# A two-layer trunk on one core: the down projections of the FFNs as products on the upper and the lower 64 rows of the array, each half with a PSUM bank of its own

## The chip, the cores and the metric

The kernel runs on one core of one Trainium2 chip. The metric is the time of one execution on the device in microseconds (us); of several runs the median is given. The core has four engines that matter here: TensorE (PE in the profile, its weight loads PEld) multiplies, VectorE (DVE) and ScalarE (ACT) work on tiles, and the DMA queue of SyncE (SP) brings weights from DRAM. TensorE writes only to PSUM, which has eight banks of 128 partitions x 512 float32 values.

## What is computed

A decoder trunk of two layers on 256 tokens of width 2048. Layer 0 mixes tokens by window means, layer 1 by latent attention; each layer ends with a SwiGLU FFN with a hidden width of 5632. All is float32. Cut to the part that the change touches:

```python
D_MODEL, SEQ, DEPTH = 2048, 256, 2
FFN_DIM = ((8 * D_MODEL // 3 + 255) // 256) * 256        # 5632

def swiglu(h, w_gate, w_up, w_down):
    return (jax.nn.silu(h @ w_gate) * (h @ w_up)) @ w_down

def reference(x, c, ...):
    for i in range(DEPTH):
        ...
        h = modulate(rmsnorm(x, norm_ffn[i]), shift_f, scale_f)
        x = x + gate_f[:, None, :] * swiglu(h, ffn_gate[i], ffn_up[i], ffn_down[i])
    return rmsnorm(x, final_norm)
```

## The kernel before

**Products.** Every matrix of weights is cut into units of 512 rows x 512 columns (1 MB). A unit is loaded into a buffer `raw`, split by ScalarE into a rounded upper part `hi` (line 368, type float32r) and by VectorE into the rest, `lo` (line 370). Activations are held as an upper and a lower part too. `proj_unit` (lines 387 to 393) then forms upper times upper, lower times upper and upper times lower: 3 parts x 4 row tiles of 128 x 2 tiles of 128 tokens = 24 products, each with a weight load of 128 x 128 (the activations) and 512 streamed columns (the weights of the network). The two token tiles have one bank each. In the last unit of a sum, the products of the first token tile go before those of the second; in all others they alternate.

**Banks.** All banks come from one pool of eight buffers, `ps`, and are given out as they come free.

**The FFN.** The hidden width is 11 chunks of 512. `FFN_STEPS` (line 52) is the order: `p` projects a chunk through gate and up, `t` transposes it (line 587) and splits it (lines 590 and 591), `d` sends a group of chunks through the down projection. The groups are [0, 1, 2], [3, 4, 5], [6, 7, 8] and [9, 10]; step d0 is followed at once by two transposing steps, d1 and d2 by the projection of a chunk, and d3 ends the FFN. Step `d` is `down(i)` (lines 594 to 625): for each of four blocks of 512 columns it takes two banks, adds the units of the group's chunks to them and evacuates them: in d0 ScalarE copies a bank to `x` (line 623), in d1 and d2 VectorE adds it to `x` (line 625), and in d3 it goes through `StreamEnd` to the gate and the residual sum.

**What runs beside.** Each split calls `tick`, which now and then emits a unit of "background": rows of the adaLN matrices, loaded into a `raw` buffer and summed by VectorE (lines 183 and 233). In the first FFN that is about three background units for four units of weights, in the second fewer. At times a finished background sum is folded (line 261) or spread as a gate over four banks (lines 299 and 300) by TensorE, in between the units. Splits have a raised priority in the scheduler that orders each engine's queue; each queue runs strictly in order. There are six `raw` buffers and six for `hi` and `lo` together, so three units of split weights.

Of the kernel before, what the change touches and what calls it, by code (L numbers as in the profile page):

```python
# [17 lines left out]
P = 128  # L18
# [31 lines left out]

# an FFN's order: chunk projected (p), turned (t), group of chunks through the down projection (d)
FFN_STEPS = "p0 p1 t0 p2 t1 p3 t2 p4 p5 d0 t3 t4 p6 t5 d1 p7 t6 p8 t7 p9 t8 d2 p10 t9 t10 d3".split()
GROUPS = ([0, 1, 2], [3, 4, 5], [6, 7, 8], [9, 10])
# chunks begun block by block, and the chunk before which the residual stream leaves for DRAM
BEGUN = 6
ASIDE = 5
# row tiles of the first gate that the tensor engine sums
GM_PE = (8, 10, 12, KD - 2, KD - 1)
# units of weights over which the background of a stage is spread
FFN0_UNITS, MLA_UNITS, HEAD_UNITS, WO_UNITS, FFN1_UNITS = 95, 6, 16, 8, 60  # L60
# of the background: blocks left to the last FFN, units left to attention, units of the last FFN's first block
# that go ahead of the output projection
LATE, MLA_LATE, WO_LATE = 3, 9, 3
# splits of weights that go before the end of a fold, or of a gate
FOLD_WAIT, GATE_WAIT = 2, 1
# [27 lines left out]
def tile_trunk(ctx: ExitStack, tc: tile.TileContext, a: dict, out: bass.AP):  # L93
# [33 lines left out]

    # constants and small vectors
    x = const.tile([P, NT, D], F32, name="x")
# [32 lines left out]

    # adaLN rows: acc[p, n] = sum over row tiles of w[kt*128+p, n] * silu(c); partition 0 starts at the bias
    cols = const.tile([P, 10, KD], F32, name="cols")
# [20 lines left out]

    # a gate on all partitions, with some of its row tiles summed on the idle tensor engine
    class SharedPart(Part):
# [13 lines left out]

    # the same for CH columns of shift and scale at once, two row tiles in a unit
    class BlockPart:
# [39 lines left out]
        def add_sums(self, i, rows, ones_, first, last):  # L243
            """Adds the sums over partitions of rows [..., CH] to KL columns of a bank, which only its first product clears."""
            for k in range(KL):
                n = i * KL + k
                pe.matmul(self.sums[:, n:n + 1], lhsT=rows[:, k * P:(k + 1) * P], rhs=ones_, start=first and k == 0,
                          stop=last and k == KL - 1)
# [3 lines left out]
    def folded(acc, n, fin):  # L252
        """Sums over partitions of acc [P, n]: column 32 * b + i is in row 32 * r + i of column b, for any r."""
        tr = raw_t([P, n])
        dve.transpose(tr, acc)
        part = acc[:, :n // 32]
        dve.tensor_reduce(out=part, in_=tr.rearrange("p (b j) -> p b j", j=32), axis=AX.X, op=ALU.add)

        def finish():
            pt = ps_t()  # L260
            pe.matmul(pt[:, :n // 32], lhsT=fold, rhs=part, start=True, stop=True)  # L261
            v = pt[:, :n // 32].rearrange("p (k r) -> p k r", r=4)
            for r in range(4):
                rows = slice(32 * r, 32 * r + 32)
                fin(v[rows, :, r], rows)
        pending.append((FOLD_WAIT, finish))
# [21 lines left out]
    def gate_to(name):  # L288
        def done(acc):
            # both parts of the sums, split exactly like the weights  # L290
            hi, lo = gate_t([P, D], F32R), work.tile([P, D], F32R, tag="acc", bufs=2, name=nm("acc"))
            act.activation(hi, acc, AF.Copy)
            dve.tensor_tensor(out=lo, in0=acc, in1=hi.bitcast(F32), op=ALU.subtract)

            def finish():
                banks = [ps_t() for _ in range(ND)]
                for j in range(ND):
                    js = slice(j * CH, (j + 1) * CH)
                    pe.matmul(banks[j], lhsT=ones_r, rhs=hi[:, js], start=True, stop=False)  # L299
                    pe.matmul(banks[j], lhsT=ones_r, rhs=lo[:, js], start=False, stop=True)  # L300
                gates[name] = gate_t([P, D])
                for j in range(ND):
                    act.activation(gates[name][:, j * CH:(j + 1) * CH], banks[j], AF.Copy)
            pending.append((GATE_WAIT, finish))
        return done
# [19 lines left out]

    # units of the background for a unit of weights
    rate, credit, goal = [0.0], [0.0], [10 ** 6]
# [3 lines left out]
    def hold():  # L331
        """Emit no more of the background until release()."""
        held[0] = True
# [13 lines left out]
    def plan(left, units):  # L347
        """Spread the background down to what is left over the next units of weights."""
        pump(len(background) - goal[0])
        goal[0], credit[0] = left, 0.0  # L350
        rate[0] = (len(background) - left) / units if units else 0.0

    # what follows a unit of weights, queued behind the split of the next unit, which is more pressing
    def flush(*ins):
# [7 lines left out]

    # weights: a unit of 512 rows and 512 columns, split exactly into two parts of 12 bits
    def split(r, shape):
# [22 lines left out]
    def proj_unit(banks, t_, hi, lo, first, last, toks=range(NT)):  # L387
        """Adds a unit to the banks; the products with the lower part of the weights, which is split last, come last."""
        for part in [[tok] for tok in toks] if last else [toks]:
            order = [(w, i, k, tok) for w, i in ((hi, 0), (hi, 1), (lo, 0)) for k in range(KL) for tok in part]  # L390
            for n, (w, i, k, tok) in enumerate(order):
                pe.matmul(banks[tok], lhsT=t_[:, i, k, tok * P:(tok + 1) * P], rhs=w[:, k, :],  # L392
                          start=first and n < len(part), stop=last and n >= len(order) - len(part))

    def proj(src, tiles):
# [5 lines left out]

    # statistics of the residual stream
    ssq = [None]
# [71 lines left out]

    # while an FFN runs, the residual stream waits in DRAM and x gathers the FFN's sum before the gate
    aside = {}
# [55 lines left out]

    # a projection of the hidden state, begun before all of the hidden state is known
    class Begun:
# [36 lines left out]
    def ffn(l, hT, gate_name, begun, then):  # L572
# [21 lines left out]
        def down(i):  # L594
# [6 lines left out]
            for j in range(ND):  # L601
                js = slice(j * CH, (j + 1) * CH)
                banks = [ps_t() for _ in range(NT)]
                if last and j == ND - 1:
# [9 lines left out]
                for c in g:  # L614
                    hi, lo = w_unit(wd[c * CH:(c + 1) * CH, js])
                    proj_unit(banks, mids[c], hi, lo, c == g[0], c == g[-1])
                    if last and j == ND - 1 and c == g[0]:
                        then()
                for tok in range(NT):
                    if last:  # L620
                        end.piece(banks[tok], tok, j)
                    elif i == 0:
                        act.activation(x[:, tok, js], banks[tok], AF.Copy)
                    else:
                        dve.tensor_tensor(out=x[:, tok, js], in0=banks[tok], in1=x[:, tok, js], op=ALU.add)  # L625

# [16 lines left out]

    # rope tables with the rows of two heads on partitions; the sine has the sign of its half
    cos_t = const.tile([P, T], F32, name="cos_t")
# [31 lines left out]
    def rope_start(bank):  # L677
        """bank [128, T] holds the rows of two heads; returns what rope_end needs."""
        t_ = t2k([P, 2, T])
# [10 lines left out]

# [1 line left out]
    rope_tables()  # L692
# [19 lines left out]
    pump(KD)  # L712
    # window means less the values, of the normed stream and of a constant one
    flat = hl_t([P, len(WINDOWS), T], F32)
# [15 lines left out]

# [1 line left out]
    def sf_block(l, j, cshift, cscale, shared=False):  # L732
# [17 lines left out]
    def start_ffn(l, rstd, first, cshift, cscale, late):  # L750
        """The first chunks, block by block of the hidden state, as its shift and scale become known."""
        begun = begin(l, range(BEGUN), (0,))
# [88 lines left out]

# [1 line left out]
    pts = turned_pieces(scaled(rstd, 0, True))  # L843
# [56 lines left out]
    def keys_values(g):  # L900
        """Keys and values of four heads."""
        mem = act_t([P, 2 * KG * T], F32)
# [30 lines left out]

    # rope key, once with zeros below and once with zeros above, for both heads of a pair
    krT = const.tile([P, 2, T], F32, name="krT")
# [112 lines left out]
    for o in heads:  # L1048
        o.finish()
    # the first columns of the output projection fill the waits of the last pairs of heads  # L1050
    w_o, ob = a["w_o"][0], []
# [39 lines left out]

# [1 line left out]
    hT, begun = start_ffn(1, rstd, None, C_SF1, C_AF1, LATE)  # L1093
# [25 lines left out]
```

## Time and profile before

| | |
|---|---|
| median of 3 runs | 1966.45 us (1965.64 to 1966.51) |
| span of the profiled execution, first to last instruction | 1962.3 us |
| mean granted clock of TensorE | 0.983 |
| bytes moved by DMA | 572.66 MB, 292 GB/s on average |
| products of line 392 | 7008, in both FFNs, the attention and its projections |
| evacuations in d0 (line 623) | 16, of 0.60 us |
| evacuations in d1 and d2 (line 625) | 32, of 0.69 us |

The runs give the time of a whole execution; of the profiled one only the span between its first and last instruction is known. In the trace a product of TensorE lasts longer than the distance to the next one, since products are pipelined: what counts is the distance between starts. A merged row of the timeline gives the start of the first instruction of a run of like ones, the time from there to the end of the last, and their count. A row of a group gives busy time and mean duration, and behind the second bar the time for which the engine stood idle just before such instructions, with what ended most of it.

The down steps d0, d1 and d2 of the first FFN end near 520, 633 and 832 us of the span, those of the second near 1554, 1664 and 1864 us.

### The profile page before, as it was taken

The page shows a single profiled execution, that of the slowest core. Times are in us where ns is not written, and L with a number is a line of the kernel's source. Part 1 is how long each engine was busy: PE and PEld are TensorE (multiplying, and loading weights), DVE is VectorE, ACT ScalarE, POOL GpSimd, SP SyncE. Part 2 cuts the span into 40 slices and gives each one's busy share as a digit, 9 for nine tenths or more (in the row PEclk, how much of TensorE's full clock was granted, in tenths as well). Part 3 has the DMA queues.
Part 4 walks back from the last instruction along what each step waited for, and adds up shares of the span by engine and source line. Part 5 has one row for each costly group of instructions (what it writes and reads, how often), then busy time and mean ns, then how long its engine had stood idle before and what let it go on. Part 6 is the DMA issues. An engine that isn't in the chain of part 4 may idle for free. (4 is left out here: it accounts for less than half of the span.)

```text
span 1962.3 us, 21516 instructions
## 1 busy us (share of the span) xinstructions
PE 1853.0 (94%) x8485; PEld 1520.7 (77%) x8485; DVE 1546.4 (79%) x1312; ACT 850.0 (43%) x939; POOL 35.9 (2%) x33
## 2 busy tenths in 40 slices
PE   0489999999999999998999999999999999999998
PEld 0444888888888888886789987888888888888886
DVE  7887899998778778888989975889986566554556
ACT  3123544444443333334676744544444433343333
POOL 1000000000000000000000000000000000000000
PEclk9889999999999999999899999999999999999999
DMA  9999998898898989987888684989887667665561
GB/s 377 408 378 365 379 321 305 310 350 327 313 329 302 332 325 345 338 333 284 307 311 304 228 295 142 360 303 325 297 293 260 225 229 257 235 209 186 195 219 70
DMA packets 225184, 572.66 MB, mean 292 GB/s; under 512 B 11958, under 2 KB 16286, under 8 KB 203442
## 3 DMA queue, kind: packets, MB, share of 16 engines
q1 hardware_dynamic: 225084, 571.30, 80.9%
q8 instruction: 66, 1.08, 0.2%
q14 instruction: 34, 0.28, 0.0%
HBM read 564.97 MB, written 6.29 MB: 291 GB/s over the span
## 5 line engine op out<-in xcount | busy, mean ns | idle before, releaser
L392 PE MATMUL ps<-hl,act 128*128 128x512 f32 x7008 | 1609.5, 391 | 4.7 <-ACT act L459 2.2
L392 PEld LDWEIGHTS ps<-hl,act 128*128 128x128 f32 x7008 | 1315.1, 188 | 279.3 <-ACT act L459 4.4
L370 DVE TENSOR_TENSOR hl<-raw,hl 128x2048 fp32r<-128x2048 f32 x296 | 676.2, 2289 | 239.9 <-ACT hl L368 236.1
L368 ACT ACTIVATE hl<-raw 128x2048 fp32r<-128x2048 f32 x296 | 566.4, 1919 | 608.7 <-PE ps L392 542.1
L183 DVE SCALAR_TENSOR_TENSOR acc<-raw,s_col,acc 128x2048 f32<-128x2048 f32 x155 | 364.0, 2348 | 4.2 <-DMA raw<-in_mod_w_dram 1.6
L233 DVE SCALAR_TENSOR_TENSOR acc<-raw,s_col,acc 128x1024 f32<-128x1024 f32 x121 | 155.0, 1281 | 8.7 <-DMA raw<-in_mod_w_dram 7.2
L556 DVE TENSOR_TENSOR act<-ps,act 128x512 f32<-128x512 f32 x96 | 64.6, 687 | 14.1 <-PE ps L392 13.7
L275 PE MATMUL ps<-ones,acc 128*128 128x1 f32 x64 | 13.9, 352 | 62.8 <-DVE acc L183 39.9
L410 ACT ACTIVATE junk<-x 128x512 bf16<-128x512 f32 x40 | 25.2, 630 | 89.6 <-DVE x L526 44.1
L275 PEld LDWEIGHTS ps<-ones,acc 128*128 128x128 f32 x64 | 13.8, 332 | 64.5 <-DVE acc L183 41.4
L590 ACT ACTIVATE act<-ps 128x512 fp32r<-128x512 f32 x44 | 23.8, 596 | 61.5 <-PE ps L587 53.4
L625 DVE TENSOR_TENSOR x<-ps,x 128x512 f32<-128x512 f32 x32 | 22.1, 691 | 35.4 <-PE ps L392 35.4
L458 ACT ACTIVATE t2k<-ps,cols 128x256 f32<-128x256 f32 x64 | 33.2, 567 | 21.6 <-PE ps L444 17.0
L634 ACT ACTIVATE t2k<-ps 128x512 f32<-128x512 f32 x24 | 14.2, 593 | 64.2 <-PE ps L392 64.2
L918 PE MATMUL ps<-act,hl 128*128 128x256 f32 x128 | 37.2, 291 | 0.6 <-DVE hl L370 0.6
L919 PE MATMUL ps<-act,hl 128*128 128x256 f32 x128 | 36.7, 287 | 0.0
L920 PE MATMUL ps<-act,hl 128*128 128x256 f32 x128 | 36.1, 286 | 0.0
L591 DVE TENSOR_TENSOR act<-ps,act 128x512 fp32r<-128x512 f32 x44 | 28.2, 685 | 8.1 <-ACT act L590 8.0
L638 DVE TENSOR_TENSOR t2k<-ps,t2k 128x512 f32<-128x512 f32 x24 | 16.6, 690 | 21.3 <-PE ps L392 21.3
L444 PE MATMUL ps<-con,t2k 128*128 128x128 f32 x144 | 22.5, 306 | 11.2 <-DVE t2k L432 8.1
L784 PE MATMUL ps<-act,act 128*128 128x512 f32 x64 | 30.7, 644 | 0.9 <-issue 0.9
L554 ACT ACTIVATE act<-ps 128x512 f32<-128x512 f32 x32 | 19.1, 598 | 28.3 <-PE ps L392 28.1
(168 smaller groups left out, 955.0 us busy)
## 6 DMA issues: line engine op xcount, KB each, us to landing
raw<-in_mod_w_dram SPq DMA_DIRECT2D x128, 1024.0 KB
raw<-in_ffn_gate_dram SPq DMA_DIRECT2D x88, 1024.0 KB
raw<-in_ffn_up_dram SPq DMA_DIRECT2D x88, 1024.0 KB
raw<-in_ffn_down_dram SPq DMA_DIRECT2D x88, 1024.0 KB
raw<-in_mod_w_dram SPq DMA_DIRECT2D x128, 512.0 KB
raw<-in_kv_mod_w_dram SPq DMA_DIRECT2D x32, 1024.0 KB
raw<-in_w_o_dram SPq DMA_DIRECT2D x16, 1024.0 KB
raw<-in_w_uq_dram SPq DMA_DIRECT2D x8, 768.0 KB
```

The lines of the kernel that those rows point to most:

```text
L183: dve.scalar_tensor_tensor(out=self.acc, in0=r, scalar=s_col[:, self.kt:self.kt + 1], in1=self.acc, op0=ALU.mult, op1=ALU.add)
L233: dve.scalar_tensor_tensor(out=self.acc, in0=r[:, k], scalar=s_, in1=self.acc, op0=ALU.mult, op1=ALU.add)
L368: hi_ins = act.activation(hi, r, AF.Copy)
L370: lo_ins = dve.tensor_tensor(out=lo, in0=r, in1=hi.bitcast(F32), op=ALU.subtract)
L392: pe.matmul(banks[tok], lhsT=t_[:, i, k, tok * P:(tok + 1) * P], rhs=w[:, k, :], start=first and n < len(part), stop=last and n >= len(ord ...
L458: act.activation(full, pts[k // 2][:, k % 2, :], AF.Identity, scale=scale, bias=bias)
L556: dve.tensor_tensor(out=part, in0=banks[tok], in1=part, op=ALU.add)
L591: dve.tensor_tensor(out=m[:, 1, :, ts_], in0=v, in1=m[:, 0, :, ts_].bitcast(F32), op=ALU.subtract)
L784: pe.matmul(pt, lhsT=pooled[g // 2][:, g % 2, k, tok * P:(tok + 1) * P], rhs=wp[g][:, k, :], start=k == 0, stop=k == KL - 1)
L918: pe.matmul(pt[:, h, :], lhsT=wl(h0 + h, k), rhs=t_[:, 0, k, :], start=k == 0, stop=False)
L919: pe.matmul(pt[:, h, :], lhsT=wh(h0 + h, k), rhs=t_[:, 0, k, :], start=False, stop=False)
L920: pe.matmul(pt[:, h, :], lhsT=wh(h0 + h, k), rhs=t_[:, 1, k, :], start=False, stop=k == KL - 1)
```

## The change

A new helper, `half_rows_unit`, forms the same 24 products of a unit as 48: each is cut into the upper and the lower 64 of its 128 rows, and each half is summed in a bank of its own. `down` uses it for all groups but the last (d0, d1 and d2 of both FFNs); its blocks then hold four banks instead of two. The sum of the two halves is formed at the evacuation: in d0 ScalarE copies the bank of the upper half and VectorE adds that of the lower, in d1 and d2 VectorE adds both. The order by token tiles in the last unit of a sum is not kept there. The step d3, the projections and the attention keep `proj_unit`. Some comments are dropped as well, which shifts no instruction; later line numbers move by up to 14 lines.

```diff
+    def half_rows_unit(banks, t_, hi, lo, first, last):
+
+        order = [(w, i, k) for w, i in ((hi, 0), (hi, 1), (lo, 0)) for k in range(KL)]
+        for n, (w, i, k) in enumerate(order):
+            for tok in range(NT):
+                for half in range(2):
+                    rows = slice(half * P // 2, (half + 1) * P // 2)
+                    pe.matmul(banks[tok][half], lhsT=t_[rows, i, k, tok * P:(tok + 1) * P], rhs=w[rows, k, :],
+                              start=first and n == 0, stop=last and n == len(order) - 1)
...
             for j in range(ND):
                 js = slice(j * CH, (j + 1) * CH)
-                banks = [ps_t() for _ in range(NT)]
+                halves = not last
+                banks = [[ps_t() for _ in range(2)] if halves else ps_t() for _ in range(NT)]
...
                 for c in g:
                     hi, lo = w_unit(wd[c * CH:(c + 1) * CH, js])
-                    proj_unit(banks, mids[c], hi, lo, c == g[0], c == g[-1])
+                    unit = half_rows_unit if halves else proj_unit
+                    unit(banks, mids[c], hi, lo, c == g[0], c == g[-1])
                     if last and j == ND - 1 and c == g[0]:
                         then()
                 for tok in range(NT):
                     if last:
                         end.piece(banks[tok], tok, j)
-                    elif i == 0:
-                        act.activation(x[:, tok, js], banks[tok], AF.Copy)
-                    else:
-                        dve.tensor_tensor(out=x[:, tok, js], in0=banks[tok], in1=x[:, tok, js], op=ALU.add)
+                        continue
+                    for half, bank in enumerate(banks[tok]):
+                        if i == 0 and half == 0:
+                            act.activation(x[:, tok, js], bank, AF.Copy)
+                        else:
+                            dve.tensor_tensor(out=x[:, tok, js], in0=bank, in1=x[:, tok, js], op=ALU.add)
```

TensorE's queue where the first down step of the first FFN begins, before (`ps` are banks, `hl` the split weights, `act` the activations, which are loaded as the array's weights):

```order
L392 MATMUL ps_2683<-hl_2687,act_2157 128x512 x4
L392 MATMUL ps_2718<-hl_2725,act_2357 128x512 [waits Activation_49]
L392 MATMUL ps_2719<-hl_2725,act_2357 128x512 [waits DVE_49]
L392 MATMUL ps_2718<-hl_2725,act_2357 128x512
L392 MATMUL ps_2719<-hl_2725,act_2357 128x512
```

and now:

```order
L392 MATMUL ps_2683<-hl_2687,act_2157 128x512 x4
L402 MATMUL ps_2718<-hl_2727,act_2357 128x512 [waits Activation_49]
L402 MATMUL ps_2719<-hl_2727,act_2357 128x512 [waits DVE_49]
L402 MATMUL ps_2720<-hl_2727,act_2357 128x512 [waits DVE_49]
L402 MATMUL ps_2721<-hl_2727,act_2357 128x512 [waits DVE_49]
L402 MATMUL ps_2718<-hl_2727,act_2357 128x512
```

Two banks in turn have become four: upper and lower half of the first token tile, then of the second. The kind of product changes from whole to half rows at the first of these and stays until something else is queued between. The program order has 8 such switches in the first FFN (into and out of d0, d1 and d2, and twice more around the gate's products, which stand inside the last block of d0) and 6 in the second.

TensorE's queue at the end of d0 in the first FFN now; `t2k` are the chunks to be transposed:

```order
L402 MATMUL ps_3251<-hl_3394,act_2544 128x512
L402 MATMUL ps_3252<-hl_3394,act_2544 128x512
L597 MATMUL ps_3450<-con,t2k_2504 128x128 [waits Activation_49]
L597 MATMUL ps_3450<-con,t2k_2504 128x128 x3
L597 MATMUL ps_3457<-con,t2k_2506 128x128 [waits Activation_49]
L597 MATMUL ps_3457<-con,t2k_2506 128x128 x3
L597 MATMUL ps_3465<-con,t2k_2596 128x128 [waits Activation_49]
```

The transposes follow the last half product directly, and their banks wait for ScalarE.

VectorE's queue at the end of the first block of d2 in the first FFN, before (line 370 is a split, 183 a background sum, 498 the gate on a part of `x`):

```order
L183 SCALAR_TENSOR_TENSOR acc_4614<-raw_4804,s_col,acc_4614 128x2048 [waits DMAHW6_49,DVE_49]
L625 TENSOR_TENSOR x<-ps_4734,x 128x512 [waits PE_49]
L498 TENSOR_TENSOR x<-x,gate_3084 128x512 [waits DVE_49]
L625 TENSOR_TENSOR x<-ps_4735,x 128x512 [waits PE_49]
L370 TENSOR_TENSOR hl_4842<-raw_4839,hl_4841 128x2048 [waits DMAHW7_49,Activation_49]
```

and now (line 639 is the addition):

```order
L183 SCALAR_TENSOR_TENSOR acc_5222<-raw_5814,s_col,acc_5222 128x2048 [waits DMAHW0_49,DVE_49]
L639 TENSOR_TENSOR x<-ps_5342,x 128x512 [waits PE_49]
L639 TENSOR_TENSOR x<-ps_5344,x 128x512 [waits PE_49]
L639 TENSOR_TENSOR x<-ps_5343,x 128x512 [waits DVE_49]
L639 TENSOR_TENSOR x<-ps_5345,x 128x512 [waits DVE_49,PE_49]
L370 TENSOR_TENSOR hl_5642<-raw_5636,hl_5641 128x2048 [waits DMAHW2_49,Activation_49]
```

Four additions stand where two stood, the upper halves of both token tiles ahead of the lower ones, and the next split is queued behind them.

## The prediction

> **What bounds the kernel now.** First the page's busy times, then the six stretches of the trace in which the changed products run.
>
> ```profile
> PE 1853.0 (94%) x8485; PEld 1520.7 (77%) x8485; DVE 1546.4 (79%) x1312; ACT 850.0 (43%) x939; POOL 35.9 (2%) x33
> L392 PE MATMUL ps<-hl,act 128*128 128x512 f32 x7008 | 1609.5, 391 | 4.7 <-ACT act L459 2.2
> L392 PEld LDWEIGHTS ps<-hl,act 128*128 128x128 f32 x7008 | 1315.1, 188 | 279.3 <-ACT act L459 4.4
> ```
>
> TensorE carries the time: products of line 392 alone are 1609.5 us of the 1962.3 us span, and they waited 4.7 us in all. VectorE is second with 79%. An average says nothing of a stage, so here are the down steps whose groups are not the last, three per FFN (columns: stretch, its length, busy time and count of PE, PEld, DVE, ACT, POOL, then granted clock, DMA share, GB/s).
>
> ```profile
> 455.00:520.00 65.00, 65.00 (x288) 53.81 (x287) 50.47 (x24) 27.65 (x23) 3.63 (x2) 1.00 0.85 316
> 567.00:632.50 65.50, 65.50 (x292) 54.24 (x291) 54.98 (x31) 24.46 (x15) 1.82 (x1) 1.00 0.85 306
> 766.00:831.50 65.50, 65.50 (x290) 54.25 (x290) 56.01 (x35) 22.72 (x13) 0.00 (x0) 1.00 0.90 325
> 1488.00:1553.50 65.50, 65.50 (x297) 54.43 (x296) 37.14 (x18) 27.10 (x21) 0.00 (x0) 1.00 0.71 250
> 1598.50:1664.00 65.50, 65.50 (x290) 54.24 (x289) 40.63 (x25) 23.33 (x15) 0.00 (x0) 1.00 0.72 253
> 1799.00:1864.50 65.50, 65.50 (x291) 54.24 (x290) 38.49 (x29) 23.32 (x14) 0.00 (x0) 1.00 0.58 189
> ```
>
> PE is busy for the whole of every stretch at full clock: nothing is waited for, so here each nanosecond between two products is time of the kernel. One merged row of the timeline gives the pitch.
>
> ```profile
> 599.79 16.48 PE L392 MATMUL ps<-hl,act 128*128 128x512 f32 x72
> 983.82 0.28 PE L918 MATMUL ps<-act,hl 128*128 128x256 f32 x1
> 983.94 0.28 PE L919 MATMUL ps<-act,hl 128*128 128x256 f32 x1
> 984.06 0.28 PE L920 MATMUL ps<-act,hl 128*128 128x256 f32 x1
> ```
>
> 72 products last 16.48 us, the last for 0.39 us: (16.48 - 0.39) / 71 = 226.6 ns from start to start. Products of half the columns follow each other at 120 ns. So 256 columns cost 106.6 ns, 512 cost 213.2 ns, and 13.4 ns a product is a fixed part: the most that any rearrangement of such products could win.
>
> **The change part by part.** Products changed: 3 groups x 3 chunks x 4 column blocks x 24 x 2 FFNs = 1728; 1728 x 226.6 ns = 391.6 us, which is the six stretches. Each becomes two with 64 rows, 512 columns and a weight load of its own; 1728 products and as many loads are added. No multiplication goes. A half streams the same 512 columns, so the pair costs what it did only if its halves run side by side. The one place where the trace shows that is line 702, four products on one row each, at partitions 0, 32, 64 and 96, into four banks (two records for each, as every unrounded fp32 product has). Their like on the whole array is line 200.
>
> ```profile
> 14.22 2.55 PE L702 MATMUL ps<-t2k,ones 1*128 1x512 f32 x8 [6.20 <-DMA t2k<-in_pool_scale_dram]
> 14.19 1.00 PEld L702 LDWEIGHTS ps<-t2k,ones 1*128 1x128 f32 x8 [6.42 <-ACT junk L410]
> L702 PEld LDWEIGHTS ps<-t2k,ones x8: 281/306/333, 14.2 to 14.9; 1*128 1x128 f32 x8
> 160.98 0.59 PE L199 MATMUL ps<-acc,ones 128*128 128x512 f32 x1
> 161.41 1.02 PE L200 MATMUL ps<-raw,t2k 128*128 128x512 f32 x2
> 162.36 1.02 PE L230 MATMUL ps<-raw,s_col 128*1 128x512 f32 x2
> ```
>
> A record follows another at 161.41 - 160.98 = 0.43 us. Eight in a row would be 3.4 us; line 702 took 2.55, and its loads, at 306 ns against the usual 188, say that the array ran slowly there, perhaps at half speed, where eight would need 6.9 us. So row groups do overlap, by 3.4 / 2.55 = 1.35 at least and 2.7 at most. The eight loads fit in 1.00 us, so they overlapped too. From both sides the pair's pitch lies between 213.2 ns (fixed part hidden) and 453.2 ns (no overlap). I take 226.6, **a change of 0**: each half keeps its own stream of 512 columns and its own fixed part, and the halves lie beside each other as in line 702, the only row with row groups.
>
> The Trainium skill (TensorE: Matmul & The Clock Gate, "Measured speedup vs the span model") gives a group of row tiles one product's time and about 4 ns for each further tile. By it the pair would be an estimated 4 ns longer and the sum 1728 x 4 ns = 6.9 us higher; no run here shows such a stream.
>
> The doubled loads need room. 0.188 us is how long one lasts, not how fast they follow.
>
> ```profile
> 175.75 0.74 PEld L247 LDWEIGHTS ps<-ones,t2k 1*128 1x128 f32 x6 [0.17 <-issue]
> L247 PEld LDWEIGHTS ps<-ones,t2k x16: 181/187/187, 175.8 to 177.4; 1*128 1x128 f32 x16
> ```
>
> Six loads in 0.74 us: (0.74 - 0.187) / 5 = 110.6 ns each, and 187 ns for one row, so half the rows make a load no shorter. Two take 221 ns one behind the other: 5 ns of room in 226.6, and more if loads of the two halves overlap. Price 0; the other end is a rival below.
>
> Switches between whole-array and half-array products: by the program order 8 in the first FFN (one step is cut by the gate's products, one step is followed by a fold) and 6 in the second, 14. The nearest rows are those of line 230, which uses one column of the array: from the second L200 to L230 is 162.36 - 161.41 - 0.43 = 0.52 us, 0.09 over the pitch. Back again:
>
> ```profile
> 172.66 1.88 PE L230 MATMUL ps<-raw,s_col 128*1 128x512 f32 x4
> 174.47 1.36 PE L444 MATMUL ps<-con,t2k 128*128 128x128 f32 x8
> 407.42 1.03 PE L587 MATMUL ps<-con,t2k 128*128 128x128 f32 x8
> ```
>
> 174.47 - 172.66 - 4 x 0.43 = 0.09 us, and the eight transposes then last 1.36 us where eight of line 587 in the middle of the stream last 1.03: 0.33 more, whether by the switch or by their own operands. So 0.09 to 0.42 us each, 1.3 to 5.9 us for 14; I take 0.2 us, **+2.8 us**.
>
> The Trainium skill (TensorEngine Tiling (Array Packing), "Key Properties") says that changing the tiling mode drains TensorE. The 0.09 us at both switches agree; a program that changed mode at each product would pay it 3456 times, this one pays it 14 times.
>
> Evacuation: 8 more operations per stretch, 48 on VectorE, none more on ScalarE.
>
> ```profile
> L625 DVE TENSOR_TENSOR x<-ps,x x32: 682/692/692, 580.7 to 1864.1; 128x512 f32<-128x512 f32 x32
> L625 DVE TENSOR_TENSOR x<-ps,x 128x512 f32<-128x512 f32 x7 | 4.8, 691 | 9.3 <-PE ps L392 9.3
> L625 DVE TENSOR_TENSOR x<-ps,x 128x512 f32<-128x512 f32 x7 | 4.8, 689 | 7.8 <-PE ps L392 7.8
> L623 ACT ACTIVATE x<-ps x16: 573/600/602, 467.4 to 1553.2; 128x512 f32<-128x512 f32 x16
> ```
>
> 8 x 0.69 = 5.5 us per stretch, 33 us in all. The tightest are the second and third stretch: 54.98 and 56.01 us busy become 60.5 and 61.5 of 65.5 us, still under PE. The second and third row (line 625 in these two stretches) show what hides them: VectorE stood idle for 9.3 and 7.8 us there, only because an addition waited for its bank. Price 0, with the cover gone 8 us (rival).
>
> Banks: a step's column block holds four of the eight, and all four fill until its last products, where the last unit went token by token before and released the first bank 12 products (2.7 us) sooner. The block behind takes the other four and runs 16.3 us, the additions 4 x 0.69 = 2.8 us, so nothing waits inside a step. At a step's end the next one may want these banks: 0 to 2.8 us six times, 17 us at most; I take **+1 us**, since only the first group is followed at once by transposes, which by the order wait for ScalarE alone, and its copy is 0.60 us.
>
> Sum: 0 + 2.8 + 1 = +3.8 us. The profile was read against its span of 1962.3 us; the median of the runs, 1966.45 us, is 4.2 us more, taken as unchanged. 1966.45 + 3.8 = **1970 us**.
>
> **Rivals.** *Halves do not overlap, or only in part.* For it: line 702 has only one row per product, at the start, at a speed that the rows do not fix. Against: even at full speed 1.35 is overlap. None: 1966.45 + 391.6 + 3.8 = 2362 us; at 1.35 the pair takes 2 x 226.6 / 1.35 = 336 ns, 1728 x 109 ns = 189 us more, 2159 us.
>
> *The fixed part is paid for each half*, because load and stream share one path: 226.6 + 13.4 = 240 ns, which is also two products at the 120 ns pitch of lines 918 to 920. 1728 x 13.4 ns = 23.2 us: 1993 us. Slower than now from the point where two loads need more than 226.6 ns; the 221 ns speak against it, but closely.
>
> *The fixed part is hidden*: while one half changes weights the other streams. 213.2 ns a pair: -23.2 + 3.8 = -19.4 us, 1947 us. Nothing in the trace shows it, nothing excludes it.
>
> *VectorE becomes the bound* in the second and third stretch. If its idle time before the additions stays, 54.98 + 9.3 + 5.5 = 69.8 and 56.01 + 7.8 + 5.5 = 69.3 us against 65.5: 4.3 + 3.8 = 8.1 us, 1978 us. It decides once a lower part of weights arrives later than its products; against it, an engine that comes later to a wait waits less.
>
> **How the numbers follow.** Chances: as forecast 0.50, VectorE bound 0.08, fixed part twice 0.13, no or part overlap 0.12, fixed part hidden 0.17. 0.2% (3.9 us) is about what a measurement of this kernel tells from no change. The forecast's own range is 1.3 to 5.9 us for switches and 0 to 17 for banks, 1968 to 1989; of its 0.50, 0.27 lies within 0.2%, 0.20 above, 0.03 below. Slower: 0.20 + 0.08 + 0.13 + 0.12 = 0.53. Faster: 0.17 + 0.03 = 0.20. The range takes in the hidden fixed part (1946) and the twice-paid one with dear switches and VectorE (1966.45 + 23.2 + 5.9 + 6 = 2002); it leaves out the missing overlap, 0.12, and tails.
>
> **What would show it.** In a timeline of a down step, starts of halves on the same rows stand 226 ns apart and the two halves of a pair overlap; six stretches of 65 us; PE without idle time; VectorE at 60 to 62 us in the second and third. A pair of 240 or 213 ns, or 130 us for a stretch, makes another case right. Waits of PE for VectorE inside a step would make the fourth rival right. Wrong altogether if the rest of the program, whose products are untouched, moves by more than 3 us.

## The result: 2077.9 us, and the profile after

| | before | after |
|---|---|---|
| median of the runs | 1966.45 us | 2077.94 us (4 runs, 2075.25 to 2078.32) |
| ratio, 95% interval | | 1.0565 (1.0551 to 1.058) |
| span of the profiled execution | 1962.3 us | 2073.0 us |
| mean granted clock of TensorE | 0.983 | 0.963 |

The kernel became 5.65% slower, 111 us, far above the forecast of 1970 us and outside the range of 1946 to 2002 us that the prediction worked out. From the page of the changed kernel, first the engines' busy times, then groups (line, engine, tiles, count, busy time and mean, and behind the second bar the idle time just before them):

```profile
PE 1888.5 (91%) x10213; PEld 1543.7 (74%) x10213; DVE 1572.9 (76%) x1360; ACT 850.2 (41%) x939; POOL 33.8 (2%) x33
L392 PE MATMUL ps<-hl,act 128*128 128x512 f32 x5280 | 1227.8, 394 | 24.2 <-DVE hl L370 21.8
L183 DVE SCALAR_TENSOR_TENSOR acc<-raw,s_col,acc 128x2048 f32<-128x2048 f32 x155 | 364.1, 2349 | 190.2 <-DMA raw<-in_kv_mod_w_dram 107.9
L402 PE MATMUL ps<-hl,act 64*128 64x512 f32 x3456 | 414.9, 400 | 36.4 <-DVE hl L370 33.9
L639 DVE TENSOR_TENSOR x<-ps,x 128x512 f32<-128x512 f32 x80 | 51.0, 683 | 17.1 <-PE ps L402 12.2
```

TensorE now waits 36.4 us before half products and 24.2 us before whole ones of line 392, 33.9 and 21.8 us of it for the lower parts of weights that VectorE splits (line 370). VectorE is not overloaded: its busy time grew by 26.5 us, but its share of the span fell from 79 to 76%. What grew most on it is idle time ahead of the background sums of line 183, which wait for a DMA. The same line before:

```profile
L183 DVE SCALAR_TENSOR_TENSOR acc<-raw,s_col,acc 128x2048 f32<-128x2048 f32 x155 | 364.0, 2348 | 4.2 <-DMA raw<-in_mod_w_dram 1.6
```

155 sums of the same duration waited 4.2 us, and now 190.2. Next the time by stage: d0, the projections behind it, d1, the projections, d2 of the first FFN, then the three down steps of the second (columns as in the prediction's table of stretches).

```profile
453.00:512.00 59.00, 56.47 (x481) 46.75 (x480) 47.63 (x27) 24.50 (x18) 1.81 (x1) 0.97 0.89 322
512.00:594.00 82.00, 65.52 (x324) 53.56 (x322) 50.02 (x28) 25.40 (x23) 1.80 (x1) 0.85 0.69 243
594.00:694.00 100.00, 76.66 (x578) 61.25 (x578) 57.16 (x37) 24.06 (x15) 0.00 (x0) 0.86 0.63 221
694.00:841.00 147.00, 137.81 (x606) 113.08 (x606) 113.69 (x68) 51.09 (x35) 3.62 (x2) 0.98 0.84 305
841.00:923.00 82.00, 71.46 (x577) 57.90 (x576) 55.16 (x39) 23.87 (x15) 0.00 (x0) 0.92 0.74 261
1596.00:1662.00 66.00, 66.00 (x580) 54.27 (x579) 40.46 (x25) 27.25 (x20) 0.00 (x0) 1.00 0.69 239
1708.00:1774.00 66.00, 66.00 (x580) 54.38 (x579) 42.69 (x31) 24.31 (x15) 0.00 (x0) 1.00 0.67 230
1909.00:1975.00 66.00, 66.00 (x579) 54.41 (x580) 39.99 (x34) 24.13 (x15) 0.00 (x0) 1.00 0.58 189
```

In the second FFN the changed steps take what they took, with TensorE busy throughout. Most of the loss is in the first: from the start of d0 to the end of d2 it now takes 470 us, where it took 376.5 (455 to 831.5). The projections between the steps, which the change doesn't touch, lose too: the stretch from 694 to 841 was 133.5 us with a busy TensorE before. Another 16.5 us go between d2 and the second FFN (923 to 1596 us against 831.5 to 1488). Idle time is only part: of the 110.7 us by which the span grew, TensorE stands idle for 75.2 and is busy for 35.5 (1888.5 against 1853.0). In d1 it was busy for 76.7 us, where 65.5 did before, at a granted clock of 0.86.

The timeline inside d1 shows one turn of the trouble (start, length to the end of the last, engine, line; in brackets the idle time before and what ended it; SPq is the queue that issues loads):

```profile
617.84 2.35 DVE L183 SCALAR_TENSOR_TENSOR acc<-raw,s_col,acc 128x2048 f32<-128x2048 f32 x1 [6.87 <-DMA raw<-in_kv_mod_w_dram]
...
620.10 2.28 DVE L370 TENSOR_TENSOR hl<-raw,hl 128x2048 fp32r<-128x2048 f32 x1
620.22 0.37 SPq L381 DMA_DIRECT2D raw<-in_ffn_down_dram  x1
622.42 0.34 SPq L176 DMA_DIRECT2D raw<-in_kv_mod_w_dram  x1
622.44 5.74 PE L402 MATMUL ps<-hl,act 64*128 64x512 f32 x48 [2.82 <-DVE hl L370]
627.96 2.35 DVE L183 SCALAR_TENSOR_TENSOR acc<-raw,s_col,acc 128x2048 f32<-128x2048 f32 x1 [5.57 <-DMA raw<-in_kv_mod_w_dram]
630.23 2.48 DVE L639 TENSOR_TENSOR x<-ps,x 128x512 f32<-128x512 f32 x4
630.34 0.37 SPq L381 DMA_DIRECT2D raw<-in_ffn_down_dram  x1
632.62 2.28 DVE L370 TENSOR_TENSOR hl<-raw,hl 128x2048 fp32r<-128x2048 f32 x1
...
634.96 2.50 PE L402 MATMUL ps<-hl,act 64*128 64x512 f32 x10 [6.78 <-DVE hl L370]
```

The split ends at 622.38 us and frees a `raw` buffer; at 622.42 the next background load is issued into it; the sum that needs it stands next in VectorE's queue and starts at 627.96, 5.5 us later. The split that TensorE waits for (632.62) stands behind that sum, although its weights were loaded earlier. A sum and a split together now take 627.96 - 617.84 = 10.1 us, while the 24 products of a unit take 24 x 0.2266 = 5.4 us.

Why that order arises is read from the queues. SyncE's loads up to one background load of d2, and VectorE's queue with only its splits and sums left in (`raw` are the six load buffers in turn; the number tells loads apart):

```
SyncE    L381 raw_5636<-in_ffn_down   L176 raw_5638<-in_mod_w
         L381 raw_5701<-in_ffn_down   L176 raw_5703<-in_mod_w
         L381 raw_5758<-in_ffn_down   L381 raw_5812<-in_ffn_down
         L176 raw_5814<-in_mod_w
VectorE  L183 sum   raw_5638
         L370 split raw_5525
         L183 sum   raw_5703
         L370 split raw_5579
         L183 sum   raw_5814
         L370 split raw_5636
```

The sum of `raw_5814` stands ahead of four splits whose weights were loaded before it: 5636, 5701, 5758 and 5812. These four hold four of the six buffers, so the load of 5814 can go out only when one of the two instructions just ahead of its own sum has given its buffer back: a ring. Counting for each sum that is emitted in a down step how many splits, up to its own unit's, stand behind it: before, 32 of 38 had 0 and six had 4; after, 23 have 3 or 4 and five have 5. In the first FFN's down steps none was above 0 before. In the second the six already stood four ahead before, and four or five after, and nothing is lost there: that few sums and a DMA share of 0.58 to 0.69 leave room for it is argued, not tried.

Queue and trace can be joined sum by sum, and in the changed kernel's first FFN the wait grows with that count:

| splits behind a sum | sums | mean idle time of VectorE before it |
|---|---|---|
| 0 or 1 | 12 | 0.0 us |
| 2 | 8 | 0.35 us |
| 3 | 19 | 1.1 us |
| 4 | 13 | 2.4 us |
| 5 | 18 | 5.6 us |

With five behind it, five of the six buffers are held, and VectorE stands idle for its load from issue to landing, as in the timeline above.

### The profile page after: what moved, and what is told of

The parts are those of the page before. It is cut to its first block, busy times and chain, and to the rows that moved or that the text cites. A ratio compares the mean times of both kernels' runs of the same rounds, so it can differ in the third digit from the quotient of the medians.

```text
span 2073.0 us, 25036 instructions
## 1 busy us (share of the span) xinstructions
PE 1888.5 (91%) x10213; PEld 1543.7 (74%) x10213; DVE 1572.9 (76%) x1360; ACT 850.2 (41%) x939; POOL 33.8 (2%) x33
## 5 line engine op out<-in xcount | busy, mean ns | idle before, releaser
L392 PE MATMUL ps<-hl,act 128*128 128x512 f32 x5280 | 1227.8, 394 | 24.2 <-DVE hl L370 21.8
L392 PEld LDWEIGHTS ps<-hl,act 128*128 128x128 f32 x5280 | 997.8, 190 | 236.3 <-DVE hl L370 25.2
L183 DVE SCALAR_TENSOR_TENSOR acc<-raw,s_col,acc 128x2048 f32<-128x2048 f32 x155 | 364.1, 2349 | 190.2 <-DMA raw<-in_kv_mod_w_dram 107.9
L402 PE MATMUL ps<-hl,act 64*128 64x512 f32 x3456 | 414.9, 400 | 36.4 <-DVE hl L370 33.9
L402 PEld LDWEIGHTS ps<-hl,act 64*128 64x128 f32 x3456 | 339.3, 192 | 111.1 <-DVE hl L370 37.7
L639 DVE TENSOR_TENSOR x<-ps,x 128x512 f32<-128x512 f32 x80 | 51.0, 683 | 17.1 <-PE ps L402 12.2
L173 POOL MEMSET acc<- 128x2048 f32 x10 | 18.0, 1808 | 834.8 <-PE ps L261 437.7
L454 PEld LDWEIGHTS ps<-con,t2k 128*128 128x128 f32 x144 | 18.4, 153 | 16.2 <-DVE t2k L442 10.2
```

The source lines that it names most:

```text
L183: dve.scalar_tensor_tensor(out=self.acc, in0=r, scalar=s_col[:, self.kt:self.kt + 1], in1=self.acc, op0=ALU.mult, op1=ALU.add)
L402: pe.matmul(banks[tok][half], lhsT=t_[rows, i, k, tok * P:(tok + 1) * P], rhs=w[rows, k, :], start=first and n == 0, stop=last and n == le ...
L454: pe.transpose(pt[:, kk, tok * P:(tok + 1) * P], pieces[tok][:, (2 * h2 + kk) * P:(2 * h2 + kk + 1) * P], ident)
L639: dve.tensor_tensor(out=x[:, tok, js], in0=bank, in1=x[:, tok, js], op=ALU.add)
```

## The experiments

The theory: the half products are as fast as forecast, and the loss is VectorE's new order, with sums ahead of splits. Rivals: the half products or the four banks cost it; the 48 additions cost it; the loss grows in proportion to how far ahead a sum stands, with no part for the loads.

**pinned.** The changed kernel, but in the first FFN each background sum is queued behind the lower split of its unit (`pin` is true there).

```diff
     def split(r, shape):
-        tick()
+        pinned = pin[0]
+        if not pinned:
+            tick()
...
             lo_ins = dve.tensor_tensor(out=lo, in0=r, in1=hi.bitcast(F32), op=ALU.subtract)
+        if pinned:
+            with tc.issue_after(lo_ins.ins):
+                tick()
```

> The changed kernel, but in the first FFN each background sum is queued on VectorE behind the lower-part split of the unit with which it is emitted (an order of issue, no new wait). Halves, banks and additions stay. Theory (the queue order of VectorE is the cause): the loss of 111 us goes; 1964 to 1972 us, and PE has no idle time in the down steps. Rival A (48 more additions on VectorE): stays above 2050 us. Rival B (four banks held by each block): stays above 2050 us. Rival C (the half products themselves, their switches, their loads): stays above 2050 us.

1966.91 us, ratio 1.001 (1.0001 to 1.0019). Its groups, and its stretches of d1 and d2:

```profile
L399 PE MATMUL ps<-hl,act 128*128 128x512 f32 x5280 | 1217.9, 391 | 3.1 <-ACT act L476 2.4 <-DVE hl L372 0.7
L409 PE MATMUL ps<-hl,act 64*128 64x512 f32 x3456 | 393.8, 387 | 0.0
```

```profile
567.00:633.00 66.00, 66.00 (x584) 54.44 (x582) 59.22 (x38) 24.51 (x15) 0.00 (x0) 1.00 0.86 308
767.00:833.00 66.00, 66.00 (x580) 54.17 (x579) 63.95 (x45) 25.78 (x15) 0.00 (x0) 1.00 0.94 346
```

All half products are there, and all additions, and nothing waits before a half product. VectorE is busy for 59.2 and 64.0 of 66 us and still holds nobody up. Putting the order back takes the whole 111 us away.

**four_banks.** The changed kernel with its four banks, copies and additions, but whole rows: 24 products a unit, which take the two banks of their token tile in turn.

```diff
-                for half in range(2):
-                    rows = slice(half * P // 2, (half + 1) * P // 2)
-                    pe.matmul(banks[tok][half], lhsT=t_[rows, i, k, tok * P:(tok + 1) * P], rhs=w[rows, k, :],
-                              start=first and n == 0, stop=last and n == len(order) - 1)
+                pe.matmul(banks[tok][n % 2], lhsT=t_[:, i, k, tok * P:(tok + 1) * P], rhs=w[:, k, :],
+                          start=first and n < 2, stop=last and n >= len(order) - 2)
```

> Whole rows again, 24 products for a unit, but each token tile sums its products in two banks in turn, and the additions and copies are those of the changed kernel. The planned order of sums and splits comes out as in the kernel before. Theory (queue order): 1964 to 1972 us. Rivals A (additions) and B (banks): 2050 to 2080 us. Rival C (half products): 1964 to 1972 us like the theory, so this run only tells the theory from A and B.

1966.01 us, ratio 0.9999 (0.9989 to 1.0009). Its queue has the sums exactly as far ahead as the kernel before. Four banks and 48 more additions cost nothing that shows; the additions wait for their banks, as before:

```profile
L637 DVE TENSOR_TENSOR x<-ps,x 128x512 f32<-128x512 f32 x80 | 51.1, 684 | 37.4 <-PE ps L400 32.2 <-ACT x L635 5.2
```

**no_lower.** The changed kernel without the additions of the lower halves: it leaves out half of each sum of d0 to d2.

```diff
-                        else:
+                        elif half == 0:
                             dve.tensor_tensor(out=x[:, tok, js], in0=bank, in1=x[:, tok, js], op=ALU.add)
```

> The changed kernel without the additions of the lower halves (their banks are filled and not read, which leaves out half of three down steps in each FFN). VectorE has its old number of instructions, the sums still stand up to five splits ahead. Theory (queue order): stays at 2040 to 2080 us. Rival A (additions): 1964 to 1975 us.

2078.18 us, ratio 1.0572 (1.0556 to 1.0588): with 48 fewer operations on VectorE the whole loss stays, and so does the wait of the sums (203.4 us):

```profile
L183 DVE SCALAR_TENSOR_TENSOR acc<-raw,s_col,acc 128x2048 f32<-128x2048 f32 x155 | 364.1, 2349 | 203.4 <-DMA raw<-in_kv_mod_w_dram 118.2 <-DMA raw<-in_mod_w_dram 80.8 <-issue 1.3
```

**second_only.** Half rows only in the second FFN (`halves = not last and l == 1`).

> Half-row products only in the second FFN; the first FFN is that of the kernel before. In the order, sums of the second FFN stand four to five splits ahead both with this kernel and with the kernel before. Theory: no loss, since there are few sums and the DMA has room there; 6 switches of 0.2 us, 1964 to 1970 us. Rival (the half products cost something in each FFN that the first hides under its waits): 1975 to 2020 us.

1966.41 us, ratio 1.0002 (0.9993 to 1.0012). 864 pairs in three stretches move the time by nothing that can be measured.

**sums_ahead1, 2 and 3.** The reverse test on the kernel before, with no half product at all: from d0 to the last projection of the first FFN each sum gets queued ahead of earlier splits, so that two, three or four stand behind it (in the changed kernel it is three, four or five for 50 of the 70 sums of the first FFN). It is an ordering rule for the queue alone, with no semaphore; the diff is that of sums_ahead3, and the others have 1 and 2 for the 3.

```diff
         def add(self, r):
-            dve.scalar_tensor_tensor(out=self.acc, in0=r, scalar=s_col[:, self.kt:self.kt + 1],
-                                     in1=self.acc, op0=ALU.mult, op1=ALU.add)
+            sum_ins = dve.scalar_tensor_tensor(out=self.acc, in0=r, scalar=s_col[:, self.kt:self.kt + 1],
+                                               in1=self.acc, op0=ALU.mult, op1=ALU.add)
+            if ahead[0] and len(queued) >= 3:
+                tc.add_manual_dep(queued[-3].ins, sum_ins.ins.name,
+                                  mybir.DependencyInfo(mybir.DependencyClass.NoSync, mybir.DependencyReason.DATA), reason='order')
...
             lo_ins = dve.tensor_tensor(out=lo, in0=r, in1=hi.bitcast(F32), op=ALU.subtract)
+        if ahead[0]:
+            queued.append(lo_ins)
```

> The kernel before, whole rows, two banks, no further additions; only VectorE's queue is changed: from d0 to p10 of the first FFN each lower-part split is queued behind the background sum that comes at least two units later (in the order that is four splits ahead, where the changed kernel has two to five). Theory (queue order): the loss appears with no half product at all, 2040 to 2120 us, with PE waiting for line 370 and VectorE waiting for the sums' loads. Rivals A, B and C: 1964 to 1972 us.

> As sums_ahead3 (whole rows, only VectorE's queue changed), but a sum stands two splits ahead, not four. Theory (a ring of six raw buffers: weights that wait for their split behind a sum hold buffers, and the sum's own load gets one only when a split or sum ahead of it has run): with two held, four buffers are left to load ahead, so little or no loss, 1964 to 1985 us. Rival (any sum ahead of its split costs, by its place in the queue): about half of the 88 us of sums_ahead3, 2000 to 2020 us.

> The same with three splits ahead. Theory (ring of buffers): three buffers left, 1970 to 2025 us, clearly less than the 2053.6 us of four ahead, and more than two ahead; the loss rises faster than the number of splits. Rival (by its place in the queue): about 3/4 of 88 us, 2025 to 2040 us.

| splits behind a sum | median | ratio |
|---|---|---|
| 2 | 1982.8 us | 1.0088 (1.007 to 1.0106) |
| 3 | 1980.16 us | 1.0077 (1.0061 to 1.0092) |
| 4 | 2053.61 us | 1.0447 (1.0432 to 1.0463) |

With four behind it, the kernel before shows the changed kernel's picture. TensorE's group, then the sums:

```profile
L400 PE MATMUL ps<-hl,act 128*128 128x512 f32 x7008 | 1633.2, 394 | 63.9 <-DVE hl L374 61.4 <-ACT act L467 2.2
L184 DVE SCALAR_TENSOR_TENSOR acc<-raw,s_col,acc 128x2048 f32<-128x2048 f32 x155 | 364.1, 2349 | 141.7 <-DMA raw<-in_kv_mod_w_dram 86.8 <-DMA raw<-in_mod_w_dram 48.1 <-DMA acc<-in_kv_mod_b_dram 3.7
```

The same two groups with three behind it:

```profile
L400 PE MATMUL ps<-hl,act 128*128 128x512 f32 x7008 | 1614.4, 391 | 13.3 <-DVE hl L374 10.8 <-ACT act L467 2.4
L184 DVE SCALAR_TENSOR_TENSOR acc<-raw,s_col,acc 128x2048 f32<-128x2048 f32 x155 | 363.9, 2348 | 53.4 <-DMA raw<-in_kv_mod_w_dram 33.4 <-DMA raw<-in_mod_w_dram 13.1 <-DMA acc<-in_kv_mod_b_dram 3.7
```

The loss jumps between three and four, which fits six buffers and not a loss in proportion. But two behind cost as much as three, which the theory had not expected. The traces narrow it down: from d0 to the last projection TensorE has just two pauses of over 2 us with two behind, 3.8 us at 515.3 and 6.0 us at 879.0, and with three, 3.4 us at 460.9 and 6.0 us at 872.7. They stand near the ends of the stretch in which the order was changed, while with four behind the pauses are spread over all of it. So two or three behind seem to cost only where one order gives way to the other; what makes these two pauses stays open.

**short_loads and ahead3_short.** If the wait is for the load that the ring holds back, shorter loads take it away. In the first FFN the background loads bring 512 of the 2048 columns, and the sums take these four times; three quarters of those rows are left out. First on the changed kernel, then on sums_ahead3.

```diff
+            if short[0]:
+                sync.dma_start(r[:, :CH], self.w[self.kt * P:(self.kt + 1) * P, :CH])
...
+            if short[0]:
+                r = r[:, :CH].rearrange("p (o n) -> p o n", o=1).to_broadcast([P, ND, CH])
```

> The changed kernel, but the background sums of the first FFN load only 512 of the 2048 columns of each row tile and sum these four times over (which leaves out three quarters of those adaLN rows); VectorE's instructions and their order stay, sums are still four to five splits ahead. Theory (VectorE waits for the loads of sums that stand ahead of splits): the cycle of a sum and a split in the worst step, 10.1 us, of which 5.5 is the load from issue to landing, falls to about 8; 1985 to 2035 us. Rival (the place in the queue costs by itself, not by the load): stays at 2065 to 2085 us.

> sums_ahead3 (whole rows, sums four splits ahead, 2053.6 us) with the loads of the first FFN's background sums cut to 512 of 2048 columns, summed four times over (three quarters of those adaLN rows are left out); VectorE's instructions and how far the sums stand ahead stay the same, which short_loads did not keep. Theory (VectorE waits for the sum's load, which cannot start before an instruction just ahead of the sum has freed a buffer): the part of the wait that is transfer goes, the part that is latency stays; 1975 to 2020 us. Rival (the place in the queue costs by itself, the load is only where the wait shows): 2040 to 2060 us.

short_loads: 2040.92 us, ratio 1.0382 (1.0366 to 1.0399), above what was expected. It isn't a clean test: with the shorter loads the queue comes out with sums still further ahead (in the down steps eleven have five splits behind them, where the changed kernel has five). ahead3_short keeps the order of sums_ahead3 but for a few sums (58 of them instead of 54 have four behind), and gives 1970.09 us, ratio 1.0023 (1.0013 to 1.0032), below its range: 83.5 of sums_ahead3's 88 us are gone.

```profile
L410 PE MATMUL ps<-hl,act 128*128 128x512 f32 x7008 | 1612.6, 391 | 5.9 <-DVE hl L384 3.5 <-ACT act L477 2.2
L194 DVE SCALAR_TENSOR_TENSOR acc<-raw,s_col,acc 128x2048 f32<-128x2048 f32 x155 | 364.0, 2348 | 38.3 <-DMA raw<-in_kv_mod_w_dram 19.2 <-DMA raw<-in_mod_w_dram 13.1 <-DMA acc<-in_kv_mod_b_dram 3.6
```

The sums still wait, but 38.3 us instead of 141.7, and TensorE waits for the splits 3.5 us instead of 61.4. So the order hurts through the load. The short loads are less traffic as well; but sums_ahead3 kept the DMA busy for 0.77 to 0.79 in the down steps, less than the 0.85 to 0.90 of the kernel before, whose sums waited 4.2 us in all.

**half_columns.** 48 products a unit as in the changed kernel, but each with all 128 rows and half of the 512 columns: a test of the rival that the fixed part is paid twice, and of what the planner, the scheduler that orders the queues, counts. The copies and additions are of half the size to match; the cut below leaves them out.

```diff
-                    rows = slice(half * P // 2, (half + 1) * P // 2)
-                    pe.matmul(banks[tok][half], lhsT=t_[rows, i, k, tok * P:(tok + 1) * P], rhs=w[rows, k, :],
+                    ns = slice(half * CH // 2, (half + 1) * CH // 2)
+                    pe.matmul(banks[tok][half][:, ns], lhsT=t_[:, i, k, tok * P:(tok + 1) * P], rhs=w[:, k, ns],
```

> As many products as the changed kernel, but each on all 128 rows and 256 of the 512 columns, the two halves side by side in the result; four banks, twice as many copies and additions of half the size. The planned order of sums and splits comes out as in the kernel before. Theory (the queue order costs, not the number of products and loads): only the fixed part is paid twice, 240 instead of 226.6 ns a pair, 1728 x 13.4 = 23 us: 1982 to 1998 us. Rival (twice as many products and loads disturb VectorE or the queues in the first FFN): 2040 us or more.

1986.0 us, ratio 1.0104 (1.0089 to 1.0119), and in a merged row of its timeline 102 products:

```profile
599.79 12.40 PE L402 MATMUL ps<-hl,act 128*128 128x256 f32 x102
```

(12.40 - 0.28) / 101 = 120 ns each, 240 a pair: the price of the rival, paid by half columns and not by half rows. Its queue has the sums as far ahead as the kernel before, with as many products as the changed kernel. So the order doesn't follow from the number of products. It fits a planner that prices a product by its streamed columns: 48 x 512 for half rows, twice the 24 x 512 of before, while 48 x 256 is the same. With down steps twice as long in the plan, splits, which need a free `hl` buffer, seem due late, and sums, whose loads seem to be there long since, go ahead. This reading of the planner is argued from the queues of four_banks, half_columns and the changed kernel; its prices were not seen.

No version here is faster than the kernel before.

## Why the prediction was wrong

**The step that failed is "Evacuation"**, with its "Price 0, with the cover gone 8 us". It asked what the 48 additions cost and what hides them, and took the rest of VectorE's queue as unchanged: the sum, 0 + 2.8 + 1, has no term for a new order there, and that term measured 111 us (2077.9 against 1966.9 us of pinned). The additions themselves cost nothing that shows (no_lower, four_banks, pinned). But the change also moved what stands around them: the background sums went ahead of the splits through most of the first FFN. The queue at the end of d2's first block, which stands ahead of the prediction with four additions in place of two, has that very sum in its first row: before it is the sum of the unit just split, now it is `raw_5814`, four splits early. The row was read for the additions; it should have been read for which load each sum waits on.

**The fourth rival** had the right wait (TensorE for the lower parts of weights) with the wrong cause and size. It let VectorE run out of time, for 8 us; VectorE had time left, 42.8 us idle in d1 alone, and spent it waiting for loads. The groups of VectorE in d1 (594 to 694 us), and TensorE's half products there:

```profile
L370 DVE TENSOR_TENSOR hl<-raw,hl 128x2048 fp32r<-128x2048 f32 x10 | 22.8, 2282 | 0.0
L183 DVE SCALAR_TENSOR_TENSOR acc<-raw,s_col,acc 128x2048 f32<-128x2048 f32 x9 | 21.2, 2351 | 39.0 <-DMA raw<-in_kv_mod_w_dram 39.0
L639 DVE TENSOR_TENSOR x<-ps,x 128x512 f32<-128x512 f32 x12 | 7.4, 680 | 0.0
L402 PE MATMUL ps<-hl,act 64*128 64x512 f32 x576 | 76.7, 428 | 23.3 <-DVE hl L370 23.3
```

39.0 us of idle time stand before nine sums, none before splits or additions.

**A change of 0 for the pair: right.** d1 of the second FFN, one step of 288 pairs between other work:

```profile
1707.11 1.03 PE L597 MATMUL ps<-con,t2k 128*128 128x128 f32 x8
1708.08 65.58 PE L402 MATMUL ps<-hl,act 64*128 64x512 f32 x576
1773.59 6.67 PE L392 MATMUL ps<-hl,act 128*128 128x512 f32 x28
```

The step's first half product starts at 1708.08 and the last ends 65.58 us later. With 0.39 us for the last product, (65.58 - 0.39) / 287 = 227.1 ns from pair to pair. That excludes three rivals: missing overlap (336 ns or more), the fixed part twice (240) and hidden (213). The room for the loads was enough.

**Switches: right; banks: right as long as the order holds.** The gate's products inside d0, in the timeline of pinned (lines 299 and 300 are whole rows):

```profile
499.75 8.55 PE L409 MATMUL ps<-hl,act 64*128 64x512 f32 x74
508.23 0.50 PE L299 MATMUL ps<-gate,ones 128*128 128x512 f32 x1
508.57 0.40 PE L300 MATMUL ps<-acc,ones 128*128 128x512 f32 x1
508.80 0.39 PE L299 MATMUL ps<-gate,ones 128*128 128x512 f32 x1
...
509.95 0.39 PE L300 MATMUL ps<-acc,ones 128*128 128x512 f32 x1
510.27 2.12 PE L409 MATMUL ps<-hl,act 64*128 64x512 f32 x15
```

The first whole product is followed after 0.34 us, the next after 0.23; the last is followed after 0.32. In the unrounded starts a switch lengthens two distances, to 319 and 339 ns on the way out of the half products and to 319 and 335 ns on the way back, against 227: 0.2 us each, as taken. pinned as a whole, with all 14 switches and every bank, is 1.3 us over the kernel before (0.2 to 3.7 by its interval), where the forecast had 3.8.

In the changed kernel itself one wait for a bank is far over the 0 to 2.8 us of the prediction. The same gate's products stop after their first four:

```profile
525.24 1.28 DVE L639 TENSOR_TENSOR x<-ps,x 128x512 f32<-128x512 f32 x2
525.98 0.79 PE L299 MATMUL ps<-gate,ones 128*128 128x512 f32 x1 [12.65 <-DVE x L639]
```

The gate needs four banks while its block holds four, so it waits for the additions of the block before, which stand on VectorE behind two sums that wait 3.7 and 5.0 us for their loads. The prediction's "nothing waits inside a step" left the gate out. In pinned the wait is gone, and no_lower, which has no such additions, loses as much without it; so it is one more effect of the order, not a price of the banks.

**The clause "Wrong altogether if the rest of the program, whose products are untouched, moves by more than 3 us"** is the one that came true: the projections between the down steps lost time as well, since the order of the queue doesn't end with the step that caused it.

## What to carry to other kernels

Where a planner fills queues that run in order, a change in how one engine's work is cut can reorder the queue of another; so compare the queues of all engines over a whole stage, and for each instruction that waits on a load ask whether the buffer of that load is freed only just ahead of it. If an engine's share falls while the bound engine waits for it, look at the idle time in its own queue first. An order on which the kernel depends should be pinned: one explicit rule took back 111 us here.

## What the runs showed of the hardware

- Two products on 64 rows each, in banks of their own, overlap fully: in pinned their starts stand 3 to 4 ns apart and a pair takes 226 to 227 ns, as one product of 128 rows. Half the rows cost as much as all, so halves win nothing by themselves. The Trainium skill (TensorE: Matmul & The Clock Gate, "Measured speedup vs the span model") adds about 4 ns for the further tile. The trace has such a distance between the halves' starts, but not in the pitch of a stream: 1728 x 4 = 6.9 us would stand in pinned's time, which is up by 1.3 us in all.
- A switch between half and whole rows costs 319 + 335 - 2 x 227 = 200 ns. The Trainium skill (TensorEngine Tiling (Array Packing), "Key Properties") says that a change of mode drains TensorE; the longer distances fit that, though no run shows that TensorE is empty in them.
- Pauses can cost more than their length: in d1 TensorE stood idle for 23.3 us and was busy for 11 us more than before, at a mean granted clock of 0.86. After the pause of 6.78 us that ends at 634.96 the granted clock is 0.50, and pairs follow each other at 427 ns for about 3 us before they are back at 227; after the 2.82 us that end at 622.44 the 24 pairs follow each other at (5.74 - 0.39) / 23 = 0.233 us.
